# Attention scores in a hybrid encoder block: low parts of the keys on all 128 partitions, negated queries, a vector minimum as bias, an fp32r mask product and joint reciprocals

## The chip, the core and the metric

The kernel runs on one core of one Trainium2 chip. The metric is the device time of one execution in microseconds. A core has a matrix engine (TensorE, PE in the profile; its weight loads are shown apart as PEld), a vector engine (VectorE, DVE), an activation engine (ScalarE, ACT), a general engine (GpSimd, POOL), and SyncE (SP), which here only issues transfers. Each engine works through its own queue in order.

## What is computed

The reference is one layer: a normalised input goes through one wide projection into three token mixers (pooling, gated linear attention, forgetting attention), then an output projection with residual, a SwiGLU feed-forward block and a last norm. The change is in the forgetting attention alone (8 heads of 64, 1024 tokens):

```python
def fox_mixer(q, k, v, f_logit, b_f):
    ...
    qh = heads(q) * (Dh ** -0.5)
    logf = jax.nn.log_sigmoid(f_logit + b_f)
    F = jnp.cumsum(logf, axis=1).transpose(0, 2, 1)
    ...
        s = jnp.einsum('bhqd,bhkd->bhqk', qb, kh) + Fb[..., None] - F[:, :, None, :]
        s = jnp.where(kpos[None, :] <= qpos[:, None], s, -jnp.inf)
        p = jax.nn.softmax(s, axis=-1)
        return jnp.einsum('bhqk,bhkd->bhqd', p, vh)
```

## The kernel before

Float32 values are split into a high and a low part of type fp32r; a product is the sum of high x high, high x low and low x high (`gemm`, L135 to L141). The first norm and its transpose give `hT`. Then come the projections in channel layout (`project`, L245), each 128 output channels wide, in two chunks of 512 tokens with 24 matmuls of 128x512 each, then gated linear attention and pooling, then the forgetting attention, the output projection, the second norm and the feed-forward block, which is over half the time and isn't touched.

The forgetting attention goes by four pairs of heads `p` (0 to 3). `fox_qk(p)` (L447) makes from the projections `zq` and `zk`, for each head `a` of the pair, a tile `Q[a]` with the high parts of the queries on 64 partitions and the low parts on the other 64, and a tile `K[a]` with the high parts of the keys on both halves: ACT writes them on the head's own partitions and POOL copies them to the other half (L461). The low parts of the keys of both heads share one tile `kl`, each on its 64 partitions (DVE, L460).

`fox_item(p, a, m, ...)` (L464) handles 256 queries of one head in two blocks of 128 (`i`). For a block with `W` keys, in one part of up to 512 columns or in two, a score tile `s` in PSUM is the sum of `Q` x `K` over 128 partitions (L489), `Q` x `kl` over the head's 64 partitions (L490) and, for the part with the diagonal, identity x mask in bfloat16 (L492). A vector instruction (L494) subtracts the running sum of the forget gates `fb`, writes the result to `pb` and keeps its maximum `mx`. DVE makes the bias `nb` from it (L498), ACT takes the exponential and its sum `l` (L499), DVE the reciprocal `rl` (L500); the rows are scaled on POOL for `i` = 0 (L502) and on DVE for `i` = 1 (L504). Then 128x128 blocks are transposed on PE into `pt` (L514), split into parts `pp` by ACT and DVE (L516, L517) and multiplied with the values `V` into `o` (L528). There are 32 items, 64 blocks, 96 score tiles and 64 mask products.

What runs between these steps is chosen by a scheduler at build time, which orders each engine's queue by its own estimate of times; while one pair attends, the projections of the next pair (`zq`, `zk`), values (`psv`) and, in the last pair, the first half of the output projection (`pxa`, weights `wo`, inputs `mix`) stand among the score instructions on PE.

Tiles come from 33 numbered slots, handed out in the order of the program and given back by hand (`G`, `free`, L51 to L59); a tile that gets a slot waits for the last use of the tile that had it. The weights `wo` and the inputs `mix` of the output projection get the slots of `hT`, whose last readers are the projections of the keys of pair 3 (`zk3p`). The low part of a weight is made on POOL (`split_w`, L115).

Of the kernel before, what the change touches and what calls it, by code (L numbers as in the profile page):

```python
# [11 lines left out]
BF16 = mybir.dt.bfloat16  # L12
# [20 lines left out]
def tile_hybrid_block(ctx: ExitStack, tc, x, w_fv, w_gv, w_zt, w_o, w_gu, w_down, ln, w_pool, w_a3, chans, b_f, consts, out):  # L33
# [9 lines left out]
    # 4 KB slots, handed out in program order; each tile is given back by hand  # L43
# [36 lines left out]
    identb = cst.tile([P, P], BF16, name="identb")  # L80
    maskb = cst.tile([P, P], BF16, name="maskb")
# [3 lines left out]
    Ft = cst.tile([P, 64], F32, name="Ft")  # L85
# [3 lines left out]
    def rstd_of(ss, n, name):  # L89
        """(ss / n + eps) ** -0.5 on a small tile."""  # L90
# [7 lines left out]
    def rstd_D(ms, parts, name):  # L98
        """the same from one or two parts of the mean square."""
# [35 lines left out]
    def gemm(ps, terms):  # L135
        """accumulates products of split operands: hi*hi + hi*lo + lo*hi."""
# [7 lines left out]
    def new_T(name):  # L144
        """[k pair][chunk][part] tiles: two k tiles by 512 tokens."""
# [6 lines left out]
    def norm_T(src, gain, hT, tb, name, sq, pts, parts=1):  # L152
        """rmsnorm of one 128-token tile, transposed into the high and low parts hT."""
# [74 lines left out]
    POOL.tensor_copy(identb, ident)  # L228
    POOL.tensor_copy(maskb, cc[:, 0:128])
# [5 lines left out]
    def log_sigmoid(items):  # L235
        """dst = min(x, 0) - ln(1 + exp(-|x|)) for (x, dst, temporary)."""
# [15 lines left out]
    # the mixers' outputs wait in memory for the output projection  # L252
# [11 lines left out]
    def decays():  # L264
        """log decays and forget gates, summed along the tokens."""
# [19 lines left out]
        pf = PS("o", "pf")  # L285
        for tb in range(NT):
            PE.transpose(pf[:, tb * 8:(tb + 1) * 8], Fc[0:8, tb * P:(tb + 1) * P], ident[0:8, 0:8])
        DVE.tensor_copy(Ft, pf[:, 0:64])
# [33 lines left out]
    def gla_state(j, kt):  # L322
        """the running state before each chunk."""
# [108 lines left out]
    def fox_values(q):  # L432
        """values of two head pairs in token layout: [pair][4 token tiles][128, tile, head, high | low]."""
# [13 lines left out]
    def fox_qk(p):  # L447
        """per head: queries [high; low] and keys [high; high] on 128 partitions, and the keys' low parts."""
        Q, K = ([G(f"{n}{p}_{a}", F32R) for a in range(2)] for n in "qk")
        kl = G(f"kl{p}", F32R)  # L450
        own = [slice(0, 64), slice(64, 128)]
        for csl, ps in project(2 * p, f"zq{p}"):
            for a in range(2):
                ACT.activation(Q[a][own[a], csl], ps[own[a]], AF.Copy, scale=0.125)
                DVE.scalar_tensor_tensor(out=Q[a][own[1 - a], csl], in0=ps[own[a]], scalar=0.125, in1=f(Q[a][own[a], csl]),
                                         op0=ALU.mult, op1=ALU.subtract)
        for csl, ps in project(2 * p + 1, f"zk{p}"):
            for a in range(2):
                ACT.activation(K[a][own[a], csl], ps[own[a]], AF.Copy)
                DVE.tensor_tensor(out=kl[own[a], csl], in0=ps[own[a]], in1=f(K[a][own[a], csl]), op=ALU.subtract)  # L460
                POOL.tensor_copy(K[a][own[1 - a], csl], f(K[a][own[a], csl]))  # L461
        return Q, K, kl

    def fox_item(p, a, m, ops, fb, V):  # L464
        """one head, 256 queries."""
        Q, K, kl = ops[0][a], ops[1][a], ops[2]
        nm = f"{p}_{a}_{m}"
        rows = slice(64 * a, 64 * a + 64)
        Pb = []
        for i in range(2):  # L470
# [5 lines left out]
            mx, nb, l, rl = (S(f"{n_}{nm}_{i}") for n_ in ("mx", "nb", "l", "rl"))  # L476
# [7 lines left out]
            top = -3.0e38  # L484
            for h in range(nh):
# [11 lines left out]
            ft = Ft[:, qb * 8 + 2 * p + a:qb * 8 + 2 * p + a + 1]  # L497
# [7 lines left out]
            Pb.append(pb)  # L505
# [507 lines left out]
```

## Time and profile before

| | us |
|---|---|
| Three runs | 1203.73, 1209.89, 1211.15 |
| Median | 1209.89 |
| Span of the profiled execution, first to last instruction | 1204.8 |
| of it, TensorE busy | 1173.7 |
| VectorE, ScalarE, GpSimd busy | 827.4, 530.5, 378.0 |
| Attention stage (226 to 488 us): TensorE busy | 261.6 of 262 |

The profile is of one execution, and gives its span alone, which lies among the three times. Times in it count from the first instruction. Matmuls overlap: one may be recorded as 0.39 us while the next starts 0.23 us after it, so what a matmul takes from the engine is read from the distance between two starts, not from its own duration. An instruction's line is that of the kernel before.

### The profile page before, as it was taken

To read this page: it belongs to the slowest core of one execution; us is meant where nothing else is said; L and a number is where in the kernel's file an instruction comes from. 1 tells how busy PE (TensorE), PEld (TensorE's weight loads), DVE (VectorE), ACT (ScalarE), POOL (GpSimd) and SP (SyncE) were. 2 spreads that over 40 slices of the span, in tenths; PEclk is the share of its full clock that TensorE was granted. 3 is DMA by queue.
4 is the path that set the end of the run, shared out by engine and by line. 5 is a ranking of instruction groups with operands and counts; after the bars stand their busy time and mean duration, and the time that the engine had idled before them with its cause. 6 is when DMAs were issued, how large, how long until landed. Compare 5 with 4: busy or idle time off the path is not lost.

```text
span 1204.8 us, 16026 instructions
## 1 busy us (share of the span) xinstructions
PE 1173.7 (97%) x5936; PEld 960.1 (80%) x5936; DVE 827.4 (69%) x1425; ACT 530.5 (44%) x965; POOL 378.0 (31%) x269
## 2 busy tenths in 40 slices
PE   6999999999999999998999999999999999999995
PEld 6888788778887777886888888888888888888874
DVE  7567622477656776678998778676776595876684
ACT  6362121455555644557444334443443343344353
POOL 2163121332222621451022220122202380760873
PEclk9999999999999999999999999999999999999998
DMA  6121111111121621231153332323224588333123
GB/s 244 35 71 53 54 36 53 53 40 47 45 59 54 209 90 38 96 132 53 53 152 113 112 108 77 131 95 116 95 90 148 212 318 292 98 111 115 61 97 139
DMA packets 53565, 126.34 MB, mean 105 GB/s; under 512 B 4792, under 2 KB 10344, under 8 KB 53488
## 3 DMA queue, kind: packets, MB, share of 16 engines
q1 hardware_dynamic: 53056, 123.75, 30.6%
q0 software_dynamic: 432, 1.57, 0.4%
q8 instruction: 46, 0.75, 0.3%
q14 instruction: 31, 0.25, 0.1%
HBM read 93.03 MB, written 32.28 MB: 104 GB/s over the span
## 4 chain that ended last, share of the span: by engine, by line
PE 88%; DVE 4%; DMA 3%; issue 2%; ACT 2%; POOL 1%; SPq 0%; POOLq 0%; ACTq 0%; DVEq 0%
PE m L714 35%; PE d L920 15%; PE pxa L140 4%; PE psv L140 4%; PE o L528 3%; PE s L490 3%; PE pt L514 3%; PE s L489 1%; DMA ra<-cd 1%; PE pxb L140 1%; PE psg L140 1%; PE zq0p L140 1%; PE zk1p L140 1%; PE zq1p L140 1%; PE zq2p L140 1%
## 5 line engine op out<-in xcount | busy, mean ns | idle before, releaser
L714 PE MATMUL m<-hA_0h,wr 128*128 128x512 f32 x616 | 214.3, 390 | 0.6 <-ACT hr L645 0.5
L714 PE MATMUL m<-hA_1h,wr 128*128 128x512 f32 x616 | 214.6, 389 | 0.0
L714 PEld LDWEIGHTS m<-hA_0h,wr 128*128 128x128 f32 x616 | 115.6, 188 | 24.9 <-ACT hr L645 1.1
L714 PEld LDWEIGHTS m<-hA_1h,wr 128*128 128x128 f32 x616 | 115.7, 188 | 23.9
L920 PE MATMUL d<-hw,ha 128*128 128x512 f32 x308 | 120.4, 393 | 5.3 <-ACT hw L819 5.1
L698 ACT ACTIVATE wr<-ws 128x512 fp32r<-128x512 f32 x110 | 69.3, 631 | 119.5 <-DVE ws L697 57.0
L714 PE MATMUL m<-hA_0l,wr 128*128 128x512 f32 x308 | 119.9, 389 | 1.7 <-DVE hA_0l L675 1.7
L920 PE MATMUL d<-lw,ha 128*128 128x512 f32 x308 | 120.9, 393 | 0.7 <-DVE lw L820 0.7
L714 PE MATMUL m<-hA_1l,wr 128*128 128x512 f32 x308 | 119.8, 389 | 0.0
L920 PE MATMUL d<-hw,la 128*128 128x512 f32 x308 | 119.1, 392 | 0.0
L766 POOL TENSOR_TENSOR cg<-cu,cu 128x512 f32<-128x512 f32 x11 | 19.2, 1743 | 309.4 <-DVE cu L743 309.4
L699 DVE TENSOR_TENSOR wr<-ws,wr 128x512 fp32r<-128x512 f32 x110 | 79.2, 725 | 29.7 <-ACT wr L698 29.6
L820 DVE TENSOR_TENSOR la<-ra,ha 128x1024 fp32r<-128x1024 f32 (+1 forms) x42 | 60.2, 1438 | 34.4 <-ACT ha L819 27.1
L819 ACT ACTIVATE ha<-ra 128x1024 fp32r<-128x1024 f32 (+1 forms) x42 | 41.4, 988 | 72.3 <-DMA ra<-cd 66.1
L920 PEld LDWEIGHTS d<-hw,ha 128*128 128x128 f32 x308 | 58.2, 189 | 18.2 <-ACT hw L819 5.5
L812 POOL TENSOR_TENSOR rw<-wd,wd 128x512 f32<-128x512 f32 x33 | 55.1, 1696 | 54.1 <-PE d L920 49.6
L502 POOL TENSOR_TENSOR pb<-pb,rl 128x128 f32<-128x128 f32 (+3 forms) x32 | 33.3, 1042 | 119.9 <-DVE rl L500 107.4
L714 PEld LDWEIGHTS m<-hA_0l,wr 128*128 128x128 f32 x308 | 57.8, 188 | 14.2 <-DVE hA_0l L675 2.2
L920 PEld LDWEIGHTS d<-lw,ha 128*128 128x128 f32 x308 | 58.4, 190 | 13.4 <-DVE lw L820 1.1
L920 PEld LDWEIGHTS d<-hw,la 128*128 128x128 f32 x308 | 58.4, 190 | 12.3
L714 PEld LDWEIGHTS m<-hA_1l,wr 128*128 128x128 f32 x308 | 57.8, 188 | 12.1
L499 ACT ACTIVATE pb<-pb,nb 128x128 f32<-128x128 f32 (+3 forms) x64 | 49.4, 772 | 35.0 <-DVE nb L498 34.9
(394 smaller groups left out, 2756.2 us busy)
## 6 DMA issues: line engine op xcount, KB each, us to landing
ra<-cd SPq DMA_DIRECT2D x35, 512.0 KB, 3.8
wu<-in_w_gu_dram SPq DMA_DIRECT2D x22, 512.0 KB, 4.3
wg<-in_w_gu_dram SPq DMA_DIRECT2D x22, 512.0 KB, 3.7
wd<-in_w_down_dram SPq DMA_DIRECT2D x22, 512.0 KB, 8.0
cd<-cg SPq DMA_DIRECT2D x11, 512.0 KB, 4.6
cd<-cs SPq DMA_DIRECT2D x11, 512.0 KB, 6.8
cd<-cu SPq DMA_DIRECT2D x11, 512.0 KB, 7.7
fb<-Fd SPq DMA_DIRECT2D x8, 512.0 KB, 5.1
```

The source lines that it names most:

```text
L140: PE.matmul(ps, a, b, start=(n == 0), stop=(n == last))
L490: PE.matmul(s[:, 0:w], Q[rows, qs], kl[rows, ks], start=False, stop=not last)
L499: ACT.activation(pb[:, 0:W], pb[:, 0:W], AF.Exp, bias=nb[:, 0:1], accum_out=l)
L514: PE.transpose(pt[:, o0:o0 + P], Pb[i][:, (2 * n + b) * P:(2 * n + b + 1) * P], ident)
L528: PE.matmul(*args, start=(kb == 0 and n_ == 0), stop=(last and n_ == 1))
L698: ACT.activation(hi, src, AF.Copy)
L699: e2.tensor_tensor(out=lo, in0=src, in1=f(hi), op=ALU.subtract)
L714: PE.matmul(ps, a, b, start=(n == 0), stop=(n == 11))
L812: POOL.tensor_tensor(out=raw_[:, j * 512:j * 512 + 512], in0=wd[h0, j0 + j][:, e0, :], in1=wd[h1, j0 + j][:, e1, :], op=op)
L819: ACT.activation(hi[:, sl], src, AF.Copy)
L820: DVE.tensor_tensor(out=lo[:, sl], in0=src, in1=f(hi[:, sl]), op=ALU.subtract)
L920: PE.matmul(banks[t], a[:, o], b[:, ns], start=(j0 + j == 0 and m == 0), stop=(j0 + j == NF // 2 - 1 and m == 2))
```

## The change

Five edits, all in the forgetting attention:

- The low parts of the keys get a tile for each head, `KL[a]`, with the same numbers on both halves of the partitions, like `K[a]`; POOL makes the second half. The matmul with the low parts runs over all 128 partitions.
- The queries are scaled by -0.125 in place of 0.125, so the score tile holds the negated score; the vector instruction adds `fb` and keeps a minimum, and the exponential has scale -1 and that minimum as its bias. The instruction that made `nb` is gone, and with it the table `Ft` (8 transposes and a copy in `decays`).
- Identity and mask are fp32r in place of bfloat16 (`identr`, `maskr`), and the mask is +1e30.
- The sums of both blocks of an item stand in one tile of two columns, and one reciprocal serves both; the scaling of both follows it.
- One slot more is in use for each pair.

```diff
-    identb = cst.tile([P, P], BF16, name="identb")
-    maskb = cst.tile([P, P], BF16, name="maskb")
+    identr = cst.tile([P, P], F32R, name="identr")
+    maskr = cst.tile([P, P], F32R, name="maskr")
...
-        pf = PS("o", "pf")
-        for tb in range(NT):
-            PE.transpose(pf[:, tb * 8:(tb + 1) * 8], Fc[0:8, tb * P:(tb + 1) * P], ident[0:8, 0:8])
-        DVE.tensor_copy(Ft, pf[:, 0:64])
...
-        Q, K = ([G(f"{n}{p}_{a}", F32R) for a in range(2)] for n in "qk")
-        kl = G(f"kl{p}", F32R)
+        Q, K, KL = ([G(f"{n}{p}_{a}", F32R) for a in range(2)] for n in ("q", "k", "kl"))
...
-                DVE.tensor_tensor(out=kl[own[a], csl], in0=ps[own[a]], in1=f(K[a][own[a], csl]), op=ALU.subtract)
-                POOL.tensor_copy(K[a][own[1 - a], csl], f(K[a][own[a], csl]))
+                DVE.tensor_tensor(out=KL[a][own[a], csl], in0=ps[own[a]], in1=f(K[a][own[a], csl]), op=ALU.subtract)
+                for t_ in (K, KL):
+                    POOL.tensor_copy(t_[a][own[1 - a], csl], f(t_[a][own[a], csl]))
...
                 PE.matmul(s[:, 0:w], Q[:, qs], K[:, ks], start=True, stop=False)
-                PE.matmul(s[:, 0:w], Q[rows, qs], kl[rows, ks], start=False, stop=not last)
+                PE.matmul(s[:, 0:w], Q[:, qs], KL[:, ks], start=False, stop=not last)
                 if last:
-                    PE.matmul(s[:, w - P:w], identb, maskb, start=False, stop=True)
+                    PE.matmul(s[:, w - P:w], identr, maskr, start=False, stop=True)
...
-                                         op0=ALU.subtract, op1=ALU.max, accum_out=t_)
+                                         op0=ALU.add, op1=ALU.min, accum_out=t_)
...
-            DVE.scalar_tensor_tensor(out=nb, in0=mx, scalar=ft, in1=ft, op0=ALU.add, op1=ALU.subtract, reverse1=True)
-            ACT.activation(pb[:, 0:W], pb[:, 0:W], AF.Exp, bias=nb[:, 0:1], accum_out=l)
-            DVE.reciprocal(rl, l)
+            ACT.activation(pb[:, 0:W], pb[:, 0:W], AF.Exp, bias=mn[:, 0:1], scale=-1.0, accum_out=l[:, i:i + 1])
...
+        DVE.reciprocal(rl, l)
+        for i, (pb, W) in enumerate(zip(Pb, Ws)):
             if i == 0:
                 POOL.tensor_tensor(out=pb[:, 0:W], in0=pb[:, 0:W], in1=rl[:, 0:1].broadcast_to([P, W]), op=ALU.mult)
             else:
-                DVE.tensor_scalar(out=pb[:, 0:W], in0=pb[:, 0:W], scalar1=rl[:, 0:1], scalar2=None, op0=ALU.mult)
+                DVE.tensor_scalar(out=pb[:, 0:W], in0=pb[:, 0:W], scalar1=rl[:, 1:2], scalar2=None, op0=ALU.mult)
```

The scheduler orders the queues anew. From the second half of the output projection on, each engine's order is the one of before; in the attention it differs. Three places follow. In names such as `s0_0_1_0_0` stand the pair, the head, the item, the block and the part; the last number only counts tiles.

TensorE, where the scores of pair 0 begin. Before:

```order
L140 MATMUL zk0p1_1963<-hT3_1_0_98,zk0l_1928 128x512
L489 MATMUL s0_0_0_0_0_2003<-k0_0_1859,q0_0_1857 128x128
L490 MATMUL s0_0_0_0_0_2003<-kl0_1861,q0_0_1857 128x128
L492 LDWEIGHTS identb_73
L492 MATMUL s0_0_0_0_0_2003<-maskb_74,identb_73 128x128
L489 MATMUL s0_0_0_1_0_2016<-k0_0_1859,q0_0_1857 128x256
L490 MATMUL s0_0_0_1_0_2016<-kl0_1861,q0_0_1857 128x256
```

and now, where the three products with the high parts (L484) of these score tiles stand 13 projection matmuls earlier:

```order
L138 MATMUL zq1p0_2480<-hT2_0_0_91,zq1h_2475 128x512
L485 MATMUL s0_0_0_0_0_1996<-kl0_0_1850,q0_0_1846 128x128
L487 MATMUL s0_0_0_0_0_1996<-maskr_74,identr_73 128x128
L485 MATMUL s0_0_0_1_0_2003<-kl0_0_1850,q0_0_1846 128x256
L487 MATMUL s0_0_0_1_0_2003<-maskr_74,identr_73 128x128
L485 MATMUL s0_0_1_0_0_2032<-kl0_0_1850,q0_0_1846 128x384
L487 MATMUL s0_0_1_0_0_2032<-maskr_74,identr_73 128x128
L138 MATMUL zq1p0_2480<-hT2_0_1_92,zq1h_2475 128x512
```

What moved: the products with low parts and the mask now stand behind 13 matmuls of the next pair's query projection.

POOL, at the keys of pair 3. Before:

```order
L461 CAST k3_0_4126<-k3_0_4126 64x512
L115 TENSOR_TENSOR wo3l_4827<-wo3r_4825,wo3h_4826 128x1024
L502 TENSOR_TENSOR pb2_1_2_0_3960<-pb2_1_2_0_3960,rl2_1_2_0_3959 128x640
L567 TENSOR_TENSOR mix2_0_4841<-mr2_0_4840,mix2_0_4841 128x512
L461 CAST k3_1_4127<-k3_1_4127 64x512
```

and now:

```order
L113 TENSOR_TENSOR wo0l_4594<-wo0r_4592,wo0h_4593 128x1024
L499 TENSOR_TENSOR pb2_1_2_0_3809<-pb2_1_2_0_3809,rl2_1_2_3807 128x640
L113 TENSOR_TENSOR wo1l_4600<-wo1r_4598,wo1h_4599 128x1024
L563 TENSOR_TENSOR mix1_0_4621<-mr0_0_4616,mix1_0_4621 128x512
L563 TENSOR_TENSOR mix0_0_4617<-mr0_0_4616,mix0_0_4617 128x512
L455 CAST k3_0_3962<-k3_0_3962 64x512
L563 TENSOR_TENSOR mix3_0_4630<-mr2_0_4625,mix3_0_4630 128x512
L455 CAST kl3_0_3964<-kl3_0_3964 64x512
L499 TENSOR_TENSOR pb2_1_3_0_3880<-pb2_1_3_0_3880,rl2_1_3_3878 128x896
```

What moved: the split of the first output weight `wo0l`, which before stood ahead of all four copies of pair 3's keys, now stands between those of the first and of the second chunk.

VectorE, at the last item of pair 0's first head (pair, head, item 0, 0, 3). Before:

```order
L498 SCALAR_TENSOR_TENSOR nb0_0_3_0_2175<-mx0_0_3_0_2174,Ft_78 128x1
L455 SCALAR_TENSOR_TENSOR q1_1_2531<-zq1p1_2570,q1_1_2531 64x512
L500 RECIPROCAL rl0_0_3_0_2177<-l0_0_3_0_2176 128x1
L494 ISA pb0_0_3_1_2197,mw0_0_3_1_2201<-s0_0_3_1_0_2198,fb0_0_1994 128x512
L494 ISA mw0_0_3_1_2201 128x1
L494 ISA pb0_0_3_1_2197,mx0_0_3_1_2193<-s0_0_3_1_1_2203,fb0_0_1994,mw0_0_3_1_2201 128x512
L494 ISA mx0_0_3_1_2193 128x1
```

and now:

```order
L513 TENSOR_TENSOR pp0_0_2_0_2109<-pt0_0_2_0_2108,pp0_0_2_0_2109 128x512
L489 ISA pb0_1_0_2233,mn0_1_0_1_2240<-s0_1_0_1_0_2241,fb0_1_1990 128x256
L489 ISA mn0_1_0_1_2240 128x1
L496 RECIPROCAL rl0_0_3_2148<-l0_0_3_2147 128x2
L501 TENSOR_SCALAR pb0_0_3_1_2163<-pb0_0_3_1_2163,rl0_0_3_2148 128x1024
```

What moved: the first block's reciprocal, before ahead of the second block's reductions (L494), is now one with the second's and stands behind them and behind the next item's.

## Rows read from the trace of the kernel before

**Rows 1.** The page: busy time by engine; the chain that ended last, by engine.
```profile
PE 1173.7 (97%) x5936; PEld 960.1 (80%) x5936; DVE 827.4 (69%) x1425; ACT 530.5 (44%) x965; POOL 378.0 (31%) x269
...
PE 88%; DVE 4%; DMA 3%; issue 2%; ACT 2%; POOL 1%; SPq 0%; POOLq 0%; ACTq 0%; DVEq 0%
```

**Rows 2.** Stretches: length, busy us of each engine, granted clock, DMA share, GB/s.
```profile
226.00:488.00 262.00, 261.58 (x1443) 202.13 (x1441) 178.23 (x502) 139.16 (x291) 80.00 (x66) 0.99 0.22 70
390.00:420.00 30.00, 29.61 (x147) 21.53 (x147) 22.79 (x56) 19.78 (x38) 18.59 (x15) 0.94 0.61 209
```

**Rows 3.** Timeline of TensorE, a score tile of 512 columns: start, duration, instruction.
```profile
232.23 0.39 PE L140 MATMUL zq1p<-hT,zq1h 128*128 128x512 f32 x1
232.46 0.39 PE L489 MATMUL s<-k,q 128*128 128x512 f32 x1
232.78 0.50 PE L490 MATMUL s<-kl,q 64*128 64x512 f32 x1
233.21 0.23 PE L492 MATMUL s<-maskb,identb 128*128 128x128 bf16 x1
233.25 0.48 PE L140 MATMUL zq1p<-hT,zq1h 128*128 128x512 f32 x1
233.56 0.39 PE L140 MATMUL zq1p<-hT,zq1l 128*128 128x512 f32 x1
```

**Rows 4.** The same, a part without mask, and a tile of 128 columns.
```profile
244.29 0.37 PE L489 MATMUL s<-k,q 128*128 128x448 f32 x1
244.59 0.47 PE L490 MATMUL s<-kl,q 64*128 64x448 f32 x1
244.99 0.51 PE L528 MATMUL o<-pp,v 128*64 128x256 f32 x3
...
280.55 0.28 PE L140 MATMUL psv<-wfv_1h,hT 128*128 128x256 f32 x1
280.67 0.28 PE L140 MATMUL psv<-wfv_1l,hT 128*128 128x256 f32 x1
280.79 0.22 PE L489 MATMUL s<-k,q 128*128 128x128 f32 x1
...
281.24 0.48 PE L140 MATMUL psv<-wfv_1h,hT 128*128 128x256 f32 x2
```

**Rows 5.** Matmul groups: busy us, mean ns of one, idle before.
```profile
L528 PE MATMUL o<-pp,v 128*128 128x128 f32 x32 | 8.9, 277 | 0.0
L426 PE MATMUL py<-pd,misc 128*128 128x512 f32 x8 | 5.5, 802 | 0.0
L287 PE MATMUL pf<-ident,Fc 8*128 8x8 f32 x8 | 0.7, 204 | 0.0
```

**Rows 6.** Weight-load groups, in the same columns.
```profile
L489 PEld LDWEIGHTS s<-k,q 128*128 128x128 f32 x96 | 18.4, 192 | 2.6 <-DVE mx L494 0.7 <-DVE q L455 0.2 <-DVE nb L498 0.2
L490 PEld LDWEIGHTS s<-kl,q 64*128 64x128 f32 x96 | 17.6, 184 | 21.8 <-issue 20.7
L492 PEld LDWEIGHTS <-identb 128*128 128x128 bf16 x64 | 6.1, 96 | 10.6 <-issue 9.1
```

**Rows 7.** Groups of VectorE and GpSimd in the attention.
```profile
L498 DVE SCALAR_TENSOR_TENSOR nb<-mx,Ft 128x1 f32<-128x1 f32 x64 | 18.9, 295 | 0.9
L500 DVE RECIPROCAL rl<-l 128x1 f32<-128x1 f32 x64 | 10.4, 162 | 33.9 <-ACT pb L499 33.4
L504 DVE TENSOR_SCALAR pb<-pb,rl 128x256 f32<-128x256 f32 (+3 forms) x32 | 21.1, 659 | 0.2
L502 POOL TENSOR_TENSOR pb<-pb,rl 128x128 f32<-128x128 f32 (+3 forms) x32 | 33.3, 1042 | 119.9 <-DVE rl L500 107.4 <-PE pxa L140 6.6 <-PE psv L140 3.9
L461 POOL CAST k<-k 64x512 fp32r<-64x512 f32 x16 | 9.8, 610 | 18.6 <-ACT k L459 18.0
L115 POOL TENSOR_TENSOR zk1l<-zk1r,zk1h 128x1024 fp32r<-128x1024 f32 x1 | 2.4, 2396 | 3.8 <-ACT zk1h L114 3.8
```

**Rows 8.** Waits: who waited for whom, us in total, times, longest.
```profile
POOL wo0l L115 <- PE zk3p L140: 8.8, 1, 8.8
```

More of the change, by code (lines that the diff above doesn't have):

```diff
@@ L11 @@
 F32R = mybir.dt.float32r
-BF16 = mybir.dt.bfloat16
 I8 = mybir.dt.int8
@@ L84, in tile_hybrid_block @@
     wa = G("wa", F32R)[0:48, 0:256]
-    Ft = cst.tile([P, 64], F32, name="Ft")
     POOL.memset(mhalf, -0.5)
@@ L227, in tile_hybrid_block @@
     SP.dma_start(wpb, w_pool)
-    POOL.tensor_copy(identb, ident)
-    POOL.tensor_copy(maskb, cc[:, 0:128])
+    POOL.tensor_copy(identr, ident)
+    POOL.tensor_copy(maskr, cc[:, 0:128])
     POOL.tensor_copy(gmask, cc[:, 128:256])
@@ L453, in fox_qk @@
             for a in range(2):
-                ACT.activation(Q[a][own[a], csl], ps[own[a]], AF.Copy, scale=0.125)
-                DVE.scalar_tensor_tensor(out=Q[a][own[1 - a], csl], in0=ps[own[a]], scalar=0.125, in1=f(Q[a][own[a], csl]),
+                ACT.activation(Q[a][own[a], csl], ps[own[a]], AF.Copy, scale=-0.125)
+                DVE.scalar_tensor_tensor(out=Q[a][own[1 - a], csl], in0=ps[own[a]], scalar=-0.125, in1=f(Q[a][own[a], csl]),
                                          op0=ALU.mult, op1=ALU.subtract)
@@ L459, in fox_qk @@
                 ACT.activation(K[a][own[a], csl], ps[own[a]], AF.Copy)
-                DVE.tensor_tensor(out=kl[own[a], csl], in0=ps[own[a]], in1=f(K[a][own[a], csl]), op=ALU.subtract)
-                POOL.tensor_copy(K[a][own[1 - a], csl], f(K[a][own[a], csl]))
-        return Q, K, kl
+                DVE.tensor_tensor(out=KL[a][own[a], csl], in0=ps[own[a]], in1=f(K[a][own[a], csl]), op=ALU.subtract)
+                for t_ in (K, KL):
+                    POOL.tensor_copy(t_[a][own[1 - a], csl], f(t_[a][own[a], csl]))
+        return Q, K, KL
     def fox_item(p, a, m, ops, fb, V):
-        Q, K, kl = ops[0][a], ops[1][a], ops[2]
+        Q, K, KL = (t_[a] for t_ in ops)
         nm = f"{p}_{a}_{m}"
         rows = slice(64 * a, 64 * a + 64)
-        Pb = []
+        Pb, Ws = [], []
+        l, rl = S(f"l{nm}", 2), S(f"rl{nm}", 2)
         for i in range(2):
@@ L475, in fox_item @@
             qs = slice(qb * P, (qb + 1) * P)
-            mx, nb, l, rl = (S(f"{n_}{nm}_{i}") for n_ in ("mx", "nb", "l", "rl"))
+            mn = S(f"mn{nm}_{i}")
             if m >= 2:
@@ L483, in fox_item @@
                 pb = pb2[:, 512:1024]
-            top = -3.0e38
+            top = 3.0e38
             for h in range(nh):
@@ L489, in fox_item @@
                 PE.matmul(s[:, 0:w], Q[:, qs], K[:, ks], start=True, stop=False)
-                PE.matmul(s[:, 0:w], Q[rows, qs], kl[rows, ks], start=False, stop=not last)
+                PE.matmul(s[:, 0:w], Q[:, qs], KL[:, ks], start=False, stop=not last)
                 if last:
-                    PE.matmul(s[:, w - P:w], identb, maskb, start=False, stop=True)
-                t_ = mx if last else S(f"mw{nm}_{i}")
+                    PE.matmul(s[:, w - P:w], identr, maskr, start=False, stop=True)
+                t_ = mn if last else S(f"mw{nm}_{i}")
                 DVE.tensor_tensor_reduce(out=pb[:, ks], in0=s[:, 0:w], in1=fb[:, ks], scale=1.0, scalar=top,
-                                         op0=ALU.subtract, op1=ALU.max, accum_out=t_)
+                                         op0=ALU.add, op1=ALU.min, accum_out=t_)
                 top = t_[:, 0:1]
-            ft = Ft[:, qb * 8 + 2 * p + a:qb * 8 + 2 * p + a + 1]
-            DVE.scalar_tensor_tensor(out=nb, in0=mx, scalar=ft, in1=ft, op0=ALU.add, op1=ALU.subtract, reverse1=True)
-            ACT.activation(pb[:, 0:W], pb[:, 0:W], AF.Exp, bias=nb[:, 0:1], accum_out=l)
-            DVE.reciprocal(rl, l)
+            ACT.activation(pb[:, 0:W], pb[:, 0:W], AF.Exp, bias=mn[:, 0:1], scale=-1.0, accum_out=l[:, i:i + 1])
+            Pb.append(pb)
+            Ws.append(W)
+        DVE.reciprocal(rl, l)
+        for i, (pb, W) in enumerate(zip(Pb, Ws)):
             if i == 0:
@@ L503, in fox_item @@
             else:
-                DVE.tensor_scalar(out=pb[:, 0:W], in0=pb[:, 0:W], scalar1=rl[:, 0:1], scalar2=None, op0=ALU.mult)
-            Pb.append(pb)
+                DVE.tensor_scalar(out=pb[:, 0:W], in0=pb[:, 0:W], scalar1=rl[:, 1:2], scalar2=None, op0=ALU.mult)
         o = PS("o", f"o{nm}")
@@ L600, in tile_hybrid_block @@
         fox_attend(p, ops, V)
-        done = [f"kl{p}"] + [f"{n}{p}_{a}" for n in "qk" for a in range(2)] + [f"v{p}_{i}" for i in range(2)]
+        done = [f"{n}{p}_{a}" for n in ("q", "k", "kl") for a in range(2)] + [f"v{p}_{i}" for i in range(2)]
         if p == 1:
@@ L949, in _consts @@
     r = np.arange(P)
-    c[:, 128:256] = np.where(r[None, :] <= r[:, None], 0.0, -1e30)
+    c[:, 128:256] = np.where(r[None, :] <= r[:, None], 0.0, 1e30)
     c[:, 256:384] = (r[None, :] >= r[:, None]) & (r[None, :] // 64 == r[:, None] // 64)
```

## The prediction

> **What bounds the kernel now.** I read the page first. TensorE is busy for 97% of the span and carries 88% of the chain that ended last; no other engine is over 69% [rows 1]. That is an average, so I then looked at the attention by itself: from 226 to 488 us TensorE is busy for 261.6 of 262 us, VectorE for 178, ScalarE for 139, GpSimd for 80, and the granted clock is 0.99, nearly always the upper level of 2.4 GHz [rows 2]. The scheduler has filled every wait of the softmax chain with projections, so here the time is the sum of what the matmuls take, and a microsecond saved on another engine is worth nothing while that holds. A busy matrix engine is not one at its peak, though. So next I read the timeline for distances between starts. A projection matmul of 512 columns takes 0.23 us (232.23 to 232.46). The product with the high parts, with as many columns, takes 0.32 us, that with the low parts 0.43 us, the mask 0.04 us, and the projection behind it 0.31 us [rows 3]. The score products are thus far from the pace of the rest. The weight loads say why: TensorE's load side stood idle for 20.7 us ahead of the 96 loads of 64 rows, on nothing that the profile shows, and for 9.1 us ahead of the 64 bfloat16 loads; ahead of the 96 loads of 128 rows it was 2.6 us [rows 6]. A load on half of the rows isn't brought ahead of the running matmul; a load on all of them is.
>
> **The change part by part.** All is summed for the profiled execution, a span of 1204.8 us, with no more around it than the scatter of the runs; their median is 5.1 us higher.
>
> *TensorE.* For a 512-column tile with mask, the stretch from the first product to the start of the second projection behind is 232.46 to 233.56, 1.10 us [rows 3]. With three matmuls at the pace of their neighbours and the mask it would be 3 x 0.23 + 0.11 = 0.80, so 0.30 us goes. The mask's 0.11 is an estimate. Below it lies 0.06 (a quarter of 0.23); a 256-column product takes 0.12 (280.55 to 280.67) [rows 4]; as every load of 128 columns has to be covered, I take a value close to that. Against it stands a product that is fed in several passes: plain float32 has 802 ns for 512 columns, but the fp32r product of the mask's very shape has 277 ns, and is in no such class [rows 5]. Were the mask as slow as 0.23, 64 x 0.12 = 7.7 us would come back. For a part without mask, 448 columns take 244.29 to 244.99, 0.70 us, and would take 2 x 0.20 (0.23 x 448/512): again 0.30. For a 128-column tile it is 280.79 to 281.24, 0.45, and 0.08 on the matmul behind (0.31 less 0.23), against 3 x 0.11: 0.20 [rows 3, 4]. There are 56 tiles with a mask and more than 128 columns, 8 with 128, and 32 parts without mask: 56 x 0.30 + 8 x 0.20 + 32 x 0.30 = 28.0 us. The 8 transposes for `Ft` give 0.5 of their 0.7 us [rows 5]. Together 28.5 us, all on the path.
>
> The Trainium skill has a rule that names what the rows show: "TensorEngine Tiling (Array Packing)", Key Properties, says that a change of tiling mode drains the engine. By it the drain goes at all 96 places, which is the same sum.
>
> It also has one against the change: "TensorE: Matmul & The Clock Gate", in the part on weight-path modes, says that the fast weight load is off for float32 weights. The identity's load indeed has 96 ns in bfloat16 and 192 ns is what fp32r has here [rows 6]; by that rule alone the mask would lose 64 x 0.096 = 6.1 us. I count none of it, since today that short load is the one that isn't hidden, and the long ones are.
>
> *VectorE* loses 64 x 0.295 = 18.9 us (`nb`) and 32 reciprocals of 0.162, 5.2 us [rows 7]: 178 becomes 154 of some 234 us. It isn't the bound before or after, so I count nothing for it; without that cover, were VectorE to gate the stage, up to 24 us would show. The new reduction (add, minimum) I take to cost what subtract and maximum cost; ScalarE's exponential stays as it is.
>
> *GpSimd* gets 16 more copies of 0.61 us, 9.8 us: 80 becomes 90 of 234 us, covered as a total [rows 2, 7]. But the scores of a pair now wait for a copy of `KL` too. POOL makes it right behind that of `K`, so the first head's scores come 0.61 us later for each of 8 chunks (4 pairs, 2 chunks): between 0 and 4.9 us. Behind the waiting matmul stands all of TensorE's queue; but at pair 0 the order has put 13 projections of 0.23 us, 3 us, in front of it. I take 1 us.
>
> *Joint reciprocals.* The first transposes of an item take blocks of both halves, so they waited for the second half already. New is that POOL's scaling of the first half starts only with VectorE's of the second, and it is the slower: 1042 against 659 ns, 0.38 us, for 32 items between 0 and 12.3 us [rows 7]. Behind the late transposes queues the rest of TensorE's work, but the order has other score tiles or projections in front of nearly all of them. I take 0.5 us.
>
> *One slot more.* The tile of `wo0l` gets the next slot of `hT`, read by the second chunk of `zk3p` and no longer by the first. Before, POOL waited 8.8 us for `zk3p` with that split [rows 8]. Now the split comes a part of a chunk later (24 x 0.23 = 5.5 us), and the output projection that fills the last pair with it; in the same queue stand four more copies, 2.4 us. It meets the one stretch where POOL (18.6 of 30 us) and VectorE (22.8) are dense and the granted clock already falls, 0.94 [rows 2]. Between 0 and 7.9 us; I take 3, as pair 2 still has items to transpose then.
>
> The sum is -28.5 + 1 + 0.5 + 3 = -24 us: 1204.8 becomes 1180.8, and the median 1209.9 becomes 1186. At the bounds of the three costs (0 and 25.1 us) it is -28.5 and -3.4.
>
> **The rivals.**
>
> *Rows don't count.* If a product over 128 partitions is paced as one over 64, since the delay comes from something else (the same queries being loaded twice in a row, or accumulation into one tile), the 28 us stay. For it: the loads of 64 and 128 rows have about one duration, 184 and 192 ns. Against: only the 64-row and the bfloat16 loads have the idle time ahead [rows 6]. Time: 1209.9 less 0.5, 1209.
>
> The Trainium skill, "TensorE: Matmul & The Clock Gate", LDWEIGHTS, states that a load's time hangs on its columns and not on its rows. By that rule the change would gain nothing on TensorE; the trace agrees for the duration and not for the distances.
>
> *Half comes back.* TensorE's queue is shorter by a tenth and the softmax chain isn't, so the joint scaling (12.3 us) and a few handovers show. For it: GpSimd's scaling waited 107 us for reciprocals [rows 7]. Against: that wait cost TensorE nothing. Time: 1209.9 - 28.5 + 12.3 + 4 = 1198.
>
> *GpSimd gates the scores* (slower). The copies of `KL` stand in an in-order queue behind weight splits that wait for ScalarE: 3.8 + 2.4 us and two copies, 7.4 us, at the four second chunks, and 2.4 + 1.2 at the four first ones: 4 x 7.4 + 4 x 3.6 = 44 us [rows 7]. If TensorE stood idle for all of it: 1204.8 - 28.5 + 44 = 1220, as a median 1225. It decides from 3.6 us at each of the 8 handovers. Against it: POOL is idle for two thirds of the stage [rows 2].
>
> **How the numbers follow.** My forecast of 1186, with 1180 to 1193 of its own, gets 0.76; half comes back 0.14; rows don't count 0.06; GpSimd gates 0.04. A difference of 1% (12.1 us, 1197.8) is about what a measurement of this kernel can tell from none; the second case lies on that line and is halved. Faster: 0.76 + 0.07 = 0.83; within 1%: 0.07 + 0.06 = 0.13; slower: 0.04. The range starts at 1176, which is the lowest run less 28 us, and ends at 1200, behind the second case.
>
> **What would show it.** Right: the product with low parts starts 0.23 us ahead of the next 512-column matmul, its load group has no idle time, and the stretch of the attention is 24 to 28 us shorter with TensorE still at 99%; the feed-forward part keeps its length. Wrong: distances of 0.3 and 0.4 us as now; TensorE waiting for `kl` copies (L455 of the new kernel) or for the scaling (L499); a gap or a fallen clock at the start of pair 3, waiting for `wo`. A longer mask step would show at L487.

## The result: 8 of the 24 microseconds came

| | us | ratio to before |
|---|---|---|
| Before, median of 16 runs | 1206.9 (1203.5 to 1217.6) | |
| After, median of 16 runs | 1198.6 (1193.5 to 1205.1) | 0.9932, 95% interval 0.9917 to 0.9946 |
| Forecast | 1186 (1176 to 1200) | |

The kernel is faster by 8.3 us, 0.7%. The time lies in the range, at its far end; the forecast of 1186 was wrong, since two thirds of the gain didn't come. One execution of run 8 and one of run 11 below (1286.6 and 1436.5 us, at mean clocks of 0.85 and 0.75) lie far above the others of their kernels and are left out of all figures.

First the page of the kernel after, engines and chain, as in [rows 1]:

```profile
PE 1159.9 (97%) x5928; PEld 974.8 (81%) x5928; DVE 810.2 (67%) x1328; ACT 530.9 (44%) x965; POOL 390.9 (33%) x285
...
PE 84%; DVE 5%; DMA 3%; issue 3%; POOL 3%; ACT 2%; POOLq 0%; SPq 0%; ACTq 0%; DVEq 0%
```

TensorE is busy for 13.8 us less, and VectorE and GpSimd now hold a larger part of the chain. Then the place that the change is made for, a score tile of 512 columns with its mask, in TensorE's timeline after, to be held against [rows 3]:

```profile
247.32 0.39 PE L484 MATMUL s<-k,q 128*128 128x512 f32 x1
247.54 0.39 PE L485 MATMUL s<-kl,q 128*128 128x512 f32 x1
247.77 0.22 PE L487 MATMUL s<-maskr,identr 128*128 128x128 f32 x1
247.83 0.36 PE L484 MATMUL s<-k,q 128*128 128x320 f32 x1
...
252.12 0.22 PE L487 MATMUL s<-maskr,identr 128*128 128x128 f32 x1
252.18 0.68 PE L138 MATMUL zk1p<-hT,zk1h 128*128 128x512 f32 x2
252.69 0.39 PE L138 MATMUL zk1p<-hT,zk1l 128*128 128x512 f32 x1
```

High and low parts now start 0.22 and 0.23 us ahead of what follows (0.32 and 0.43 before), the mask 0.06, and the pair of projections behind it takes 0.51 (the `x2` in its line counts both; before it was 0.31 and about 0.23, and 0.46 would be full pace). The weight loads agree, beside [rows 6]:

```profile
L485 PEld LDWEIGHTS s<-kl,q 128*128 128x128 f32 x96 | 18.6, 194 | 0.8
L487 PEld LDWEIGHTS s<-maskr,identr 128*128 128x128 f32 x64 | 12.5, 195 | 0.7
```

The idle time ahead of the loads of the low parts fell from 21.8 to 0.8 us, that ahead of the mask's from 10.6 to 0.7. Summed over all 256 score products (distance to the next start, at most 0.46 us of each), they took 67.1 us before and take 44.4 now. So the pace came. Where did the rest go? The stretches show it. Before the attention ran from its first score at 226.9 us to its last `o` at 518.4; after, from 238.9 to 503.9. The stage is 26.5 us shorter, and begins 12 us late (not all of the 26.5 is gain, as the end of this section shows). The stretches ahead of it, TensorE alone (length, busy us, granted clock, DMA share, GB/s), first before, then after:

```profile
120.00:166.00 46.00, 44.10 (x424) 0.96 0.14 47
166.00:176.20 10.20, 10.20 (x47) 1.00 0.17 51
176.20:206.90 30.70, 30.70 (x206) 0.94 0.16 52
206.90:217.20 10.30, 10.30 (x62) 1.00 0.00 1
```

```profile
120.00:166.00 46.00, 44.11 (x403) 0.93 0.11 37
166.00:176.20 10.20, 10.20 (x38) 0.50 0.33 98
176.20:206.90 30.70, 30.70 (x187) 1.00 0.16 52
206.90:217.20 10.30, 10.30 (x41) 0.50 0.01 2
```

TensorE is busy all the time in both, but in two stretches of 10 us the granted clock is 0.50, its lower level of 1.2 GHz. That is in the gated linear attention, where no edited line runs. In all, 27.3 us ahead of the first score lie at the lower level, against 6.8 before. Half of the difference, 10 us, is the work that the lower level doesn't do; it is most of the 12. Of the 16 executions the profiled one is that with the lowest mean clock (0.979 and 1203.6 us, where the mean of all is 0.984), so it shows more of the lower level than the median has.

What TensorE did there is another order than before. The timeline of the kernel after, around the first fall:

```profile
162.46 0.33 PE L364 MATMUL po<-gv,attb 128*128 128x64 f32 x2
162.72 0.33 PE L368 MATMUL po<-St,bc 64*64 64x64 f32 x4
...
164.85 0.73 PE L138 MATMUL zgg0p<-hT,zgg0h 128*128 128x512 f32 x2
165.52 0.32 PE L368 MATMUL po<-St,bc 64*64 64x64 f32 x2
165.77 0.55 PE L364 MATMUL po<-gv,attb 128*128 128x64 f32 x2
166.25 0.48 PE L368 MATMUL po<-St,bc 64*64 64x64 f32 x4
166.66 0.69 PE L364 MATMUL po<-gv,attb 128*128 128x64 f32 x2
```

Ahead of the fall stand small products `po` and two projections. Over the whole stage the `po` now stand mostly in runs of up to 12 of one head, where before they mostly went three by three between the two heads, and the dense projections stand at other places among them. The 8 transposes for `Ft` had belonged to the same stage; without them the scheduler's estimate of times shifts, and it chooses otherwise. Busy time of the small products `po` from 121.9 to 240 us, before and after:

```profile
L370 PE MATMUL po<-gv,attb 128*128 128x64 f32 x64 | 13.2, 288 | 0.0
L374 PE MATMUL po<-St,bc 64*64 64x64 f32 x128 | 10.3, 242 | 0.0
```

```profile
L364 PE MATMUL po<-gv,attb 128*128 128x64 f32 x64 | 15.2, 324 | 0.0
L368 PE MATMUL po<-St,bc 64*64 64x64 f32 x128 | 12.9, 267 | 0.0
```

And inside the attention TensorE isn't busy throughout any more. The stage as a whole and the start of pair 3 (all engines in the order PE, PEld, DVE, ACT, POOL), to be held against [rows 2]:

```profile
239.00:504.00 265.00, 253.95 (x1548) 224.82 (x1547) 182.07 (x430) 152.07 (x319) 106.26 (x93) 0.97 0.24 77
405.00:435.00 30.00, 23.69 (x124) 19.95 (x125) 20.95 (x44) 19.02 (x36) 21.04 (x17) 0.89 0.50 167
```

11 us without TensorE in the stage, 6.3 of them in those 30 us. The first half of the output projection that used to fill them now stands partly behind the attention: from the last `o` to the feed-forward part it takes 49.6 us, where it took 37.0. So 12.6 of the 26.5 us only moved. From the first score to the end of the output projection it is 13.9 us less; the two stretches, TensorE alone, before and then after (columns as above):

```profile
226.90:554.80 327.90, 325.84 (x1779) 0.99 0.24 79
```

```profile
238.90:552.90 314.00, 302.15 (x1779) 0.98 0.25 83
```

TensorE's idle time in it rose from 2.1 to 11.9 us, and the time at the lower clock from 3.4 to 13.7.

### The profile page after: what moved, and what is told of

It is laid out like the page before. It is cut to its first block, busy times and chain, and to the rows that moved or that the text cites. A ratio compares the mean times of both kernels' runs of the same rounds, so it can differ in the third digit from the quotient of the medians.

```text
span 1201.8 us, 15933 instructions
## 1 busy us (share of the span) xinstructions
PE 1159.9 (97%) x5928; PEld 974.8 (81%) x5928; DVE 810.2 (67%) x1328; ACT 530.9 (44%) x965; POOL 390.9 (33%) x285
## 3 DMA queue, kind: packets, MB, share of 16 engines
q1 hardware_dynamic: 53056, 123.75, 30.7%
## 4 chain that ended last, share of the span: by engine, by line
PE 84%; DVE 5%; DMA 3%; issue 3%; POOL 3%; ACT 2%; POOLq 0%; SPq 0%; ACTq 0%; DVEq 0%
PE m L710 35%; PE d L916 16%; PE pxa L138 4%; PE psv L138 3%; PE o L524 3%; PE pt L510 2%; PE s L484 1%; PE zq0p L138 1%; PE zgg0p L138 1%; PE s L485 1%; DMA mr<-mixd 1%; PE psg L138 1%; PE po L364 1%; PE zq3p L138 1%; PE zgg1p L138 1%
## 5 line engine op out<-in xcount | busy, mean ns | idle before, releaser
L695 DVE TENSOR_TENSOR wr<-ws,wr 128x512 fp32r<-128x512 f32 x110 | 75.9, 696 | 26.0 <-ACT wr L694 26.0
L499 POOL TENSOR_TENSOR pb<-pb,rl 128x128 f32<-128x128 f32 (+3 forms) x32 | 38.1, 1196 | 83.4 <-DVE rl L496 66.5
L816 DVE TENSOR_TENSOR lw<-rw,hw 128x1024 fp32r<-128x1024 f32 (+1 forms) x30 | 45.7, 1535 | 27.3 <-ACT hw L815 27.2
```

Source lines behind the costliest of these rows:

```text
L695: e2.tensor_tensor(out=lo, in0=src, in1=f(hi), op=ALU.subtract)
L816: DVE.tensor_tensor(out=lo[:, sl], in0=src, in1=f(hi[:, sl]), op=ALU.subtract)
```

## The experiments

Two theories stood at the start. A: leaving `Ft` out changes TensorE's order ahead of the attention, and the granted clock with it. B: the joint reciprocals take the gain back in the attention. Each edit is shown against the kernel that its heading names; "before" is measured anew beside each group of runs, and ratios are to that. Where `Ft` is kept though nothing reads it, that is work done for nothing; all else computes the same.

**1. The change, with `Ft` still made.**

```diff
+    Ft = cst.tile([P, 64], F32, name="Ft")
...
         SP.dma_start(Fd, Fc[0:8])
+        pf = PS("o", "pf")
+        for tb in range(NT):
+            PE.transpose(pf[:, tb * 8:(tb + 1) * 8], Fc[0:8, tb * P:(tb + 1) * P], ident[0:8, 0:8])
+        DVE.tensor_copy(Ft, pf[:, 0:64])
```

> All five edits, but the table Ft is still made (8 transposes and a copy whose result nobody reads). At build, TensorE's order ahead of the attention is then that of before. Theory A (most of the missing gain is lost ahead of the attention, where the order without Ft leaves the granted clock at the lower level for 27 us in place of 7): about 10 us come back, the attention's first score starts near 227 us as before, the time is near 1188 us, ratio to before 0.984. Theory B (the gain is lost inside the attention, by the joint reciprocals and the wait for wo at pair 3): as the full change, near 1198 us, ratio 0.993.

Measured: 1188.4 us, 0.9845 (0.9819 to 0.9871). Useless work makes the kernel some 10 us faster (1198.6 without it). TensorE's order ahead of the attention is that of before again, word for word, and the first score starts at 231.1, with 13.7 us at the lower clock ahead of it: A's time came, its start near 227 only in part. From the first score on, TensorE's order is that of the kernel after, instruction by instruction, and so it is in runs 7, 8 and 11. So what these five kernels differ by comes from ahead of the attention, and not from another order in it.

**2. The same, with own reciprocals for each block as well.**

```diff
-        DVE.reciprocal(rl, l)
-        for i, (pb, W) in enumerate(zip(Pb, Ws)):
...
+            DVE.reciprocal(rl, l)
...
```

> The low parts on 128 partitions, the fp32r mask and the negated queries; Ft is still made, and each block keeps its own reciprocal. Against the run with joint reciprocals it tells what these cost. Theory A: within 3 us of that run, near 1188 us. Theory B: VectorE's scaling goes back from 1.01 to 0.66 us, TensorE no longer waits for parts pp behind it, and the time is 5 to 8 us below that run.

Measured: 1188.7, 0.9854 (0.9834 to 0.9874), no different from run 1. TensorE is busy for 254.6 of 261.0 us in the attention, against 252.8 of 261.6 in run 1. B falls as the cause of the loss.

**3. Before, with the negated queries, the minimum as bias and no `Ft`.**

```diff
-        pf = PS("o", "pf")
...
-            DVE.scalar_tensor_tensor(out=nb, in0=mx, scalar=ft, in1=ft, op0=ALU.add, op1=ALU.subtract, reverse1=True)
-            ACT.activation(pb[:, 0:W], pb[:, 0:W], AF.Exp, bias=nb[:, 0:1], accum_out=l)
+            ACT.activation(pb[:, 0:W], pb[:, 0:W], AF.Exp, bias=mx[:, 0:1], scale=-1.0, accum_out=l)
```

> The kernel before with the negated queries and the minimum as bias alone, and so without Ft; score products and reciprocals as before. Its order ahead of the attention is that of the full change. Theory A: the first score starts near 239 us, the clock is at the lower level for some 20 us more, and it is slower than before by about 10 us, 1217 us, ratio 1.008, though it does less work. Theory B: same as before within 2 us, since VectorE is not the bound.

Measured: 1216.6, 1.0086 (1.0067 to 1.0105). The edit that removes 18.9 us of VectorE's work and 8 transposes makes the kernel slower, by what A said. Order ahead of the attention: that of the kernel after. But A's mechanism isn't seen in full: the first score starts at 234.6, not near 239, and 17.1 us ahead of it are at the lower clock, where the same order had 27.3 in the kernel after.

**4. Before, with the joint reciprocals alone** (the reverse of the diff under 2).

> The kernel before with joint reciprocals alone. Theory A: within 3 us of before, as TensorE's queue covers the late scaling. Theory B: the two scalings of an item run at one time, VectorE's takes about 1.0 us in place of 0.66 and GpSimd's 1.2 in place of 1.04, and the time rises by 3 to 8 us, ratio 1.003 to 1.007.

Measured: 1210.9, 1.0046 (1.0024 to 1.0067). That is B's time. The two scalings of an item now start together, and both last longer in the mean. Groups on GpSimd and VectorE in the kernel after, to be held against [rows 7], and one pair of them in its timeline. The first two lines are of before, for the two widths of that pair:

```profile
L504 DVE TENSOR_SCALAR pb<-pb,rl 128x1024 f32<-128x1024 f32 x8 | 6.0, 749 | 0.0
L502 POOL TENSOR_TENSOR pb<-pb,rl 128x896 f32<-128x896 f32 x8 | 13.5, 1682 | 47.5 <-DVE rl L500 47.5
```

```profile
L499 POOL TENSOR_TENSOR pb<-pb,rl 128x128 f32<-128x128 f32 (+3 forms) x32 | 38.1, 1196 | 83.4 <-DVE rl L496 66.5 <-PE pt L510 10.8 <-PE s L487 3.2
L501 DVE TENSOR_SCALAR pb<-pb,rl 128x256 f32<-128x256 f32 (+3 forms) x32 | 32.0, 1006 | 0.9
```

```profile
421.10 0.17 DVE L496 RECIPROCAL rl<-l 128x2 f32<-128x2 f32 x1 [0.36 <-ACT pb L493]
...
421.30 2.27 DVE L501 TENSOR_SCALAR pb<-pb,rl 128x1024 f32<-128x1024 f32 x1
421.35 1.68 POOL L499 TENSOR_TENSOR pb<-pb,rl 128x896 f32<-128x896 f32 x1 [0.78 <-DVE rl L496]
```

VectorE's mean goes from 659 to 1006 ns (896 in run 4), GpSimd's from 1042 to 1196 in both. The Trainium skill, "SBUF — State Buffer", section "Who interferes with whom", says that the two engines share a pair of ports as a lock and names `tensor_scalar` among the instructions that can contend for it. The trace agrees: VectorE's part lasts 2.27 us here in place of 0.75, until 0.54 us behind the end of GpSimd's, which keeps its 1.68.

**5. Before, with the low parts on 128 partitions and the fp32r mask alone.**

```diff
...
-                        PE.matmul(s[:, 0:w], Q[rows, qs], kl[rows, ks], start=False, stop=not last)
+                        PE.matmul(s[:, 0:w], Q[:, qs], KL[:, ks], start=False, stop=not last)
...
-    identb = cst.tile([P, P], BF16, name="identb")
+    identb = cst.tile([P, P], F32R, name="identb")
-    maskb = cst.tile([P, P], BF16, name="maskb")
+    maskb = cst.tile([P, P], F32R, name="maskb")
```

> Before, with only the low parts on 128 partitions and the fp32r mask; subtraction, `Ft`, bias and own reciprocals as before. Theory (the pace of TensorE is the whole gain of the change): about what the kernel with negated queries and own reciprocals gave, 1186 to 1192 us, score products 44 us in place of 67. Rival (a part of the gain comes from VectorE's missing bias instruction, 18.9 us of work): 1194 to 1200 us. TensorE's order ahead of the attention is that of before, so the first score should start at 227 to 231 us.

Measured: 1190.8, 0.9864 (0.9828 to 0.9900). These two edits, with the copies and the slot that the low parts need, are the whole gain, as far as the intervals of runs 1, 2 and 5 tell.

**6. Before, with the negated queries and the minimum alone** (as 3, with `Ft` kept).

> Before, with only the negated queries and the minimum as bias; `Ft` is still made, though nothing reads it. Partner of the run that also left `Ft` out and took 1216.6 us. Theory (leaving `Ft` out costs about 10 us through TensorE's order ahead of the attention): 1200 to 1208 us, first score at 226 to 229 us. Rival (the negation itself costs it, in the attention): 1214 to 1218 us with the first score still at 227 us.

Measured: 1209.4, 1.0014 (0.9992 to 1.0037): no change in time, though somewhat above the 1200 to 1208 expected, and the first score at 231.6, not 226 to 229: this execution had 17.1 us at the lower clock ahead of it, with the order of before. So the negation is free, and against run 3 some 7 us (9 by the ratios) hang on `Ft`; the orders of these two kernels differ within the attention too.

**7 and 8. The change, with the values of pairs 0 and 1 called later**, in between or behind the two calls of `gla_out`, as another way to another order without `Ft`. The diff is that of run 7; in run 8 the line stands behind the second call.

```diff
-    V = fox_values(0)
     gla_out(0, g0[0], g0[1], g0[2], st0)
+    V = fox_values(0)
     gla_out(1, g1[0], g1[1], g1[2], st1)
```

> The changed kernel, without `Ft`, with one line moved: the values of pairs 0 and 1 (`fox_values(0)`) are now called between the two calls of `gla_out`, so that the scheduler places the dense value projections in other gaps between the small products. Theory (the 10 us hang on that order and the granted clock, not on `Ft`'s absence as such): less than 14 us at the lower clock ahead of the first score, which starts at 228 to 234 us, and 1184 to 1193 us. Rival (something else that goes with `Ft` costs the time): first score at 237 us or later and 1195 to 1202 us.

> The changed kernel with the values called behind both calls of `gla_out`; the order has runs of 12 small products of one head, like the changed kernel, but with dense projections of the values between nearly all of them. Theory (the clock falls where small products follow each other without dense ones): less than 14 us at the lower clock ahead of the first score, and 1184 to 1195 us. Rival (runs of 12 of one head are enough for the clock to fall, whatever stands between): 20 us or more at the lower clock and 1195 to 1205 us.

Measured: 1196.6, 0.9908 (0.9877 to 0.9940), and 1192.5, 0.9868 (0.9833 to 0.9902). The first score starts at 230.1 and 230.6, as the theory of run 7 said, but with 17.1 us at the lower clock ahead of it in both, more than the 14 expected; and run 7 takes a time of the rival, run 8 one of the theory. The 8 us at this place came back, and the median followed by 2 us in run 7 and by 6 in run 8.

**9 and 10. Before, with the low parts alone, and with the fp32r mask alone** (each half of the diff under 5).

> Before, with only the low parts on 128 partitions; the mask stays bfloat16. Theory (each product in another mode than its neighbours costs time at its own place): the product with low parts falls from 0.37 to about 0.19 us on average, the one with high parts behind it in the queue from 0.30 to 0.22 to 0.26, the mask stays at 0.04 with 0.08 on the matmul behind; 1189 to 1194 us. Rival (the slow distances come from the mask's type as much as from the rows): score products still above 55 us in sum and 1196 to 1202 us.

> Before, with only identity and mask in fp32r; the low parts stay on 64 partitions. Theory: the mask product grows from 0.04 to about 0.08 us and takes less from the matmul behind, so 64 places change by 0 to -0.1 us each: 1200 to 1208 us, score products 60 to 68 us in sum. Rival (fp32r after fp32r removes most of the drain): score products under 55 us and 1190 to 1198 us.

Measured: 1196.4, 0.9916 (0.9885 to 0.9946), and 1220.2, 1.0109 (1.0075 to 1.0143). The low parts alone bring the score products from 67.1 to 43.5 us, so that pace is all theirs, as the theory said, but the time is the rival's; the last 6 us up to run 5 are none of it, but waits (the distances of over 0.65 us between TensorE's starts in the attention and the output projection, less 0.2 us of work each, sum to 14.4 us in run 9 and 7.7 in run 5). The mask alone is a surprise: both theories had it harmless, and it costs 13 us, 7.1 of them in the score products (74.2 us in sum). In its profile some 4 us more lie ahead of the first score, where the order is that of before (17.1 us at the lower clock in place of 6.8), and 2 in waits. The timeline of run 10, beside [rows 3]:

```profile
237.18 0.50 PE L490 MATMUL s<-kl,q 64*128 64x512 f32 x1
237.61 0.33 PE L492 MATMUL s<-maskb,identb 128*128 128x128 f32 x1
237.77 0.44 PE L140 MATMUL zq1p<-hT,zq1h 128*128 128x512 f32 x1
238.06 0.40 PE L140 MATMUL zq1p<-hT,zq1l 128*128 128x512 f32 x1
```

Behind a product over 64 partitions the fp32r mask takes 0.16 us and the projection behind it still 0.29; in bfloat16 it was 0.04 and 0.31. Behind one over 128 it took 0.06 in the kernel after. What a product costs depends on its predecessor, and the two edits aren't a sum.

**11. The change, with the two calls of `pool_tile` exchanged**, which makes the small products alternate again in the second half of the stage.

```diff
-    pool_tile(1, us[1])
     pool_tile(0, us[0])
+    pool_tile(1, us[1])
```

> The changed kernel, without `Ft`, with two calls exchanged: `pool_tile(0)` comes ahead of `pool_tile(1)`. By the order the small products of the second `gla_out` then alternate between the two heads with the dense `zq0p` ahead of the last ones, nearly as before the change. Theory (the order of the small products ahead of the attention costs the 10 us): first score at 228 to 233 us, at most 17 us at the lower clock ahead of it, and 1186 to 1192 us. Rival (something else that goes with `Ft`): first score at 237 us or later, 1195 to 1202 us.

Measured: 1201.1, 0.9948 (0.9929 to 0.9968), a time of the rival. The theory's numbers failed: first score at 239.4 and 30.7 us at the lower clock, the first 10.2 of them from 132.1 on, after a wait of 2.9 us that began at 128.0. In the second half, where the products do alternate again, 13.6 us are at the lower level (203.8 to 210.6 and 217.4 to 224.2), against 10.2 in the kernel after. So alternation alone doesn't keep the clock up.

**12. As 8, with own reciprocals.**

> The changed kernel with two parts undone or moved: own reciprocals for each block, as before, and the values called behind both calls of `gla_out`; `Ft` stays out. Theory (the two parts that lost time are the order ahead of the attention and the joint reciprocals): scaling on VectorE near 0.65 us and on GpSimd near 1.04 us again, at most 17 us at the lower clock ahead of the first score, and 1184 to 1190 us, as good as the two best kernels so far. Rival (the joint reciprocals cost nothing beside the rest, and leaving `Ft` out costs some us in any order): 1191 to 1197 us, like the run with the values last.

Measured: 1193.3, 0.9884 (0.9864 to 0.9905), the rival's time and that of run 8. Own reciprocals give nothing here either. Ahead of the first score TensorE has the order of run 8, instruction by instruction, and yet the profiled execution has 27.3 us at the lower clock there, run 8's 17.1. TensorE in run 8, then in run 12:

```profile
132.00:146.00 14.00, 14.00 (x187) 1.00 0.34 110
146.00:153.00 7.00, 7.00 (x41) 1.00 0.01 2
153.00:169.00 16.00, 16.00 (x133) 0.89 0.12 34
```

```profile
132.00:146.00 14.00, 14.00 (x191) 1.00 0.30 93
146.00:153.00 7.00, 7.00 (x24) 0.51 0.01 2
153.00:169.00 16.00, 16.00 (x98) 0.71 0.11 33
```

All runs together; the clock is the mean over the span in a kernel's executions, the last two columns are of the profiled one:

| | us | clock | first score at | us at 1.2 GHz ahead of it |
|---|---|---|---|---|
| before | 1206.9 | 0.991 | 226.9 | 6.8 |
| after | 1198.6 | 0.984 | 238.9 | 27.3 |
| 1 with `Ft` | 1188.4 | 0.987 | 231.1 | 13.7 |
| 2 with `Ft`, own reciprocals | 1188.7 | 0.988 | 229.2 | 13.7 |
| 3 negated, no `Ft` | 1216.6 | 0.988 | 234.6 | 17.1 |
| 4 joint reciprocals | 1210.9 | 0.989 | 227.3 | 6.8 |
| 5 low parts and mask | 1190.8 | 0.986 | 231.0 | 17.1 |
| 6 negated, `Ft` | 1209.4 | 0.990 | 231.6 | 17.1 |
| 7 values between | 1196.6 | 0.981 | 230.1 | 17.1 |
| 8 values last | 1192.5 | 0.986 | 230.6 | 17.1 |
| 9 low parts | 1196.4 | 0.989 | 230.1 | 13.7 |
| 10 mask | 1220.2 | 0.989 | 231.0 | 17.1 |
| 11 pooling exchanged | 1201.1 | 0.981 | 239.4 | 30.7 |
| 12 values last, own reciprocals | 1193.3 | 0.984 | 234.7 | 27.3 |

In every row the start of the first score, less half of the last column, is between 221 and 227 us, where the starts themselves lie between 226 and 240: the clock explains most of where the attention begins. The last column is of one execution each, and is no steady property of an order: eight kernels with the order of before ahead of the attention have between 6.8 and 17.1 us there. The medians of the five kernels with the faster score products and without `Ft` (1192 to 1201) are above those of the three with it that also have the fp32r mask (1188 to 1191), but run 8 (0.987, 0.983 to 0.990) can't be told from run 5 (0.986, 0.983 to 0.990).

## Why the prediction was wrong

*TensorE's pace: right.* "Together 28.5 us, all on the path", of which 28.0 for the score products. These lost 22.7 us, and the matmul behind a mask takes 0.28 in place of 0.31, another 2. The rest shows in the sum over all matmuls: the stretch from the first score to the end of the output projection, less TensorE's idle time and less half of the time at 1.2 GHz, is 327.9 - 2.1 - 1.7 = 324.1 us before and 314.0 - 11.9 - 6.9 = 295.2 after. In run 9, with the low parts alone, it is 315.7 - 14.5 - 5.1 = 296.1 (an estimate, which counts the lower level as half the work). So 28 to 29 us of TensorE's work went. The drain that the Trainium skill has in "TensorEngine Tiling (Array Packing)", Key Properties, agrees with the trace: 0.32 and 0.43 us around a product over 64 partitions, 0.22 and 0.23 without it. What the Trainium skill, "TensorE: Matmul & The Clock Gate", LDWEIGHTS, says of columns is true of a load's duration (194 ns on 128 partitions, 184 on 64) and decides nothing here. The rival "rows don't count" is out.

*`Ft`: the step that failed.* "The 8 transposes for `Ft` give 0.5 of their 0.7 us". Leaving them out cost 9 to 10 us in place of giving 0.5 (after against run 1, two kernels with one order from the first score on), or 7 to 9 without the rest of the change (run 3 against 6). The prediction took the order as new in the attention alone and never compared TensorE's order ahead of it. In the profiled executions that order holds 20.5 us more at 1.2 GHz than before, which no term and no rival had; over all executions the mean clocks, 0.984 after and 0.987 in run 1, make some 4 of the 10 us (0.003 of a span of 1200), so the clock is shown as a part of the cost and not as all of it.

*VectorE at nothing: right.* Run 6 takes 18.9 us of `nb` away and gains nothing.

*Joint reciprocals: the mechanism was wrong, and that the size did no harm was luck.* The prediction set 1042 against 659 ns as if both stayed; started together they become 1196 and 1006. It cost 5 us alone and nothing that can be measured beside the other edits (run 1 against 2, run 8 against 12), where 0.5 was said.

*"All on the path" and "TensorE still at 99%": the second step that failed.* The prediction gave 4.5 us for all that TensorE would wait. From the first score to the end of the output projection its idle time rose from 2.1 us to 11.9 after, 9.5 in run 1 and 7.5 in run 2. The copies for `KL` aren't the cause. They cost GpSimd what was said (a group of the kernel after), GpSimd's wait for `zk3p` of [rows 8] is no longer among its waits, and none of TensorE's waits in the attention is for GpSimd; they are for VectorE and ScalarE (the list's longest below: us in total, times, longest):

```profile
L455 POOL CAST kl<-kl 64x512 fp32r<-64x512 f32 x16 | 10.0, 626 | 0.7 <-DVE kl L453 0.2
```

```profile
PE pxb L138 <- ACT mix L562: 2.8, 1, 2.8
PE s L484 <- DVE mn L489: 2.5, 2, 1.5
PE o L524 <- DVE pp L513: 2.0, 1, 2.0
PE pt L510 <- DVE pp L513: 1.4, 1, 1.4
```

So the rival "GpSimd gates" is out. As a sign of being wrong "a gap or a fallen clock at the start of pair 3" had been named, and 6.3 of the 11 us lie there, but TensorE doesn't wait for `wo` in them.

*The rival "half comes back" had the time, 1198, and the wrong cause.* Its joint scaling explains none of the median; that the softmax chain shows when TensorE's queue is shorter fits these waits, some 5 us beyond what was counted.

*The sum.* Forecast -24; measured -8.3. Run 1 gained 17.4 on its own runs of before, so 9.1 of the 15.7 that are missing are `Ft`'s. For the other 6.6 there are two causes, sized by single executions only: TensorE's waits, which in run 1 grew by 7.4 us where 4.5 were counted, and the clock, whose mean is 0.987 in run 1 where before has 0.992, which over a span of 1190 us is up to 6 us lost.

What stays open: by what rule the clock falls. Run 11 shows that alternation alone isn't it, and runs 8 and 12, like the kernel after and run 3, that one order gives 17.1 or 27.3 us. Nor does the clock account for all of `Ft`: at a mean of 0.987 five executions of the changed kernel take 1193.5 to 1198.9 us, and run 1 with 0.985 to 0.989 takes 1185.1 to 1191.6. In the profiled ones 2.2 us of the rest are TensorE's idle time in the attention (11.0 against 8.8). Nor is it shown that leaving `Ft` out must cost: run 8, with another order, got back more than half of it. The slot alone was not tried.

## What to carry to other kernels

Where a scheduler orders the queues by estimated times, compare the whole order of the bounding engine, not the stage that is edited: taking out 0.7 us of work cost 10 us through the order elsewhere, and keeping it was the better kernel (1188.4 us, with the low parts and the mask as the whole gain). Read the granted clock by stretches beside the busy share, since 100% busy at half rate looks like work. And try the parts of a change alone and together: the mask cost 13 us alone and gained beside the low parts.

## What the runs showed of the hardware

- The granted clock can fall to 1.2 GHz with no wait ahead: at 166.0 us in the kernel after, TensorE had been busy without a gap since 128.4 us, from 162.46 us on with products of 64 columns and two of 512. The Trainium skill, "TensorE: Matmul & The Clock Gate", section "Why this matters for your kernels", warns of idle gaps between bursts; here TensorE's last gap, of 1.9 us, was some 37 us back, and the lower level came all the same and held for 10.2 us, all of them busy.
- The same order of instructions, started 0.6 us earlier (run 12 against run 8), had the lower level at other places and for 10.2 us longer.
- A 128x128 fp32r product of TensorE starts 0.06 us ahead of the next when both neighbours are over 128 partitions (the kernel after; 0.08 in the mean over the 64 masks), and 0.16 behind one over 64 (run 10).
- Beside a GpSimd instruction of 128x896 a VectorE scaling of 128x1024 took 2.27 us in place of 0.75; GpSimd's took 1.68, as without it.
